# Column-group matmuls recorded as one scheduled piece, and a new list of steps, in a two-layer flow block

## The chip, the cores and the metric

The kernel runs on one core of one Trainium2 chip. The metric is the device time of one execution in microseconds (us), as the median of several runs; a profile of one execution, with every instruction's start and end, stands beside it.

## What is computed

Two layers of a block that works on 512 latent tokens and 256 context tokens of width 1024. Each layer modulates its input with rows that it makes from a condition vector (adaln), projects it to 2464 columns, sends these through four mixers (a gated convolution, latent attention, grouped attention, retention), projects back, and runs an MLP with squared ReLU. Only the latent tokens come out.

```python
def adaln(cond, w, b):
    m = (jax.nn.silu(cond) @ w + b).reshape(cond.shape[0], N_MOD, D_MODEL)
    return tuple(m[:, i, None, :] for i in range(N_MOD))

def grouped_attention(q, k, v):          # per block of 128 queries
    ...
        s = jnp.einsum('bkgqd,bksd->bkgqs', qblk, k, preferred_element_type=jnp.float32) * scale
        p = jax.nn.softmax(s, axis=-1)
        return jnp.einsum('bkgqs,bksd->bkgqd', p.astype(v.dtype), v)

def reference(...):
    for layer in range(DEPTH):           # DEPTH = 2
        last = layer == DEPTH - 1
        sh1, sc1, g1, sh2, sc2, g2 = adaln(c, w_mod[layer], b_mod[layer])
        csh1, csc1, cg1, csh2, csc2, cg2 = adaln(c_ctx[None, :], w_mod[layer], b_mod[layer])
        y_ctx, y_lat = mixing_sublayer(modulate(cx, csh1, csc1), modulate(x, sh1, sc1), ...)
        x = x + g1 * y_lat
        x = x + g2 * sq_relu_mlp(modulate(x, sh2, sc2), mlp_w1[layer], mlp_w2[layer])
        if not last:
            cx = cx + cg1 * y_ctx
            cx = cx + cg2 * sq_relu_mlp(modulate(cx, csh2, csc2), mlp_w1[layer], mlp_w2[layer])
    return rms_norm(x, final_g)
```

In the second layer no context output is needed. Everything is fp32 on the outside.

## The kernel before

Most products are made of three fp32r matmuls: an operand is split into a high and a low part (`split`), and `mm3` adds high x low, high x high and low x high in PSUM. A few products stay plain fp32. These are the ones that the change touches:

- **Modulation rows** (`mod_rows`, called for the first rows of layer 0 by `mods` and, inside layer 0's mixing, through the list `todo` by `later`). The stationary operand is `sf`, 128x32: the two condition vectors for one block of 128 inputs, padded. The contraction over 1024 inputs is 8 such blocks; they go in two sets of four, and the four of a set write to four different groups of 32 output partitions (32 array columns each) of one PSUM tile. The moving operand is a slice of `w_mod`, 256 or 512 columns wide. For 512 columns a set's weights come as two loads of 0.5 MB, two blocks each, into a class of buffers of which there are three (`raw`, `nraw = 3`).
- **Joins of attention** (`Duo.finish`). A `Duo` is a pair of heads for a pair of token tiles. `scores(k)` makes the scores of head k and their softmax, `turn(k)` transposes the probabilities on TensorE and copies them to `pts`, `finish` multiplies them with the values: for each of 6 key tiles (2 for context queries) one matmul for each head, head 0 to output partitions 0 to 63 and head 1 to 64 to 127. The units (`s_units`, `u` in the list) run a Duo's scores while the Duo before is joined.
- **Retention** (`s_ret`). In each of two pairs of heads, for each direction and segment, four fp32 matmuls with the states (128 columns) and then 8 matmuls of 64 columns, two heads by turns, in one PSUM tile.

What sets the order: no engine instruction is issued where it is written. `Plan.record` notes each as an operation with its engine (or several possible engines), a cost and its dependencies, and `Plan.schedule` then runs a list scheduling on these costs: each engine takes the ready operation that was recorded earliest, as long as buffers are free. `Plan.issue` writes the engines' programs in that order. The order of recording inside the mixing of a layer comes from the list `ORDER`: words such as `u:2` (two steps of the generator of units), `taps:4` (four taps of the convolution), `ln`, `read` (norm and readout of convolution and retention), `todo:1` (one modulation row). On a chip each engine works through its own program in order, and waits where an operand is not there.

Since every operation of `Plan` is issued on one line, nearly all instructions of the profile carry the line L646. In names, `b` is one of four PSUM tiles of 512 columns, `pp` one of two pairs of them, `m` a page of SBUF.

Of the kernel before, what the change touches and what calls it, by code (L numbers as in the profile page):

```python
# [66 lines left out]
class _Engine:  # L67
# [5 lines left out]
    def __getattr__(self, fn):  # L73
        return lambda *a, **k: self._p.record(self._n, self._r, fn, a, k)

# [35 lines left out]
class Plan:  # L111
# [7 lines left out]
    def __init__(self, tc, caps, arenas, names):  # L119
        nc = tc.nc  # L120
        self.tc, self.caps, self.arenas, self.names = tc, caps, arenas, names
        self.ahead, self.patience, self.lag = ahead, patience, 0
        self.hurry, self.bias = hurry, {"V": bV, "S": bS, "G": bG}
        self.V, self.S, self.G, self.T, self.D = [_Engine(self, n, e) for n, e in (
            ("V", nc.vector), ("S", nc.scalar), ("G", nc.gpsimd), ("T", nc.tensor), ("D", nc.sync))]
        self.ops, self.tiles = [], {}
        self.masks, self.open = {}, {}
# [66 lines left out]
    def record(self, eng, real, fn, args, kw):  # L194
        alt_kw = kw.pop("alt_kw", None) or {}
        op = _Op()
# [8 lines left out]
        for k, a in kw.items():  # L205
            if hasattr(a, "tensor"):
                (outs if k in ("out", "accum_out") else ins).append(a)
        op.alts = {}
        for e in eng:
            f = fn[e] if isinstance(fn, dict) else fn  # L210
            k = alt_kw.get(e, kw)
            op.alts[e] = (getattr(real[e] if isinstance(real, dict) else real, f), self._cost(e, f, outs, ins, k), k)
# [55 lines left out]
    def _cost_(self, eng, fn, outs, ins, kw):  # L268
# [6 lines left out]
        if eng == "D":  # L275
            big = max(n(a) * a.ap[0][1] for a in outs + ins)
            return max(big * 4 / 290.0, 60.0)
        size = n(outs[0])
        psum = any(self.tiles[a.tensor.name]["psum"] for a in outs[:1] + ins if a.tensor.name in self.tiles)
        if eng == "T":  # L280
            if fn == "transpose":
                return 109.0 if ins[0].ap[0][1] > 16 else 27.0
            if ins[0].dtype == F32:
                if ins[0].ap[-1][1] <= 64:
                    return 4 * size / 2.4 * ins[0].ap[-1][1] / 128
# [395 lines left out]
def block_kernel(ctx: ExitStack, tc: tile.TileContext, x, c, cx, c_ctx, w_mod, b_mod, w_in, w_out,  # L681
# [3 lines left out]
    nc = tc.nc  # L685
# [106 lines left out]
    def mod_rows(l, i, c0, w):  # L792
# [8 lines left out]
        for k0 in range(0, KT, 4):  # L801
# [5 lines left out]
            for k in range(4):  # L807
                T.matmul(o[32 * k:32 * k + 32], lhsT=sf[:, k0 + k], rhs=rs[k // nk][:, k % nk], start=k0 == 0, stop=k0 > 0)
# [152 lines left out]
    def mixing(l, ht, yt, todo, late=None):  # L961
# [64 lines left out]
        class Duo:  # L1026
# [43 lines left out]
            def finish(self):  # L1070
# [3 lines left out]
                for j in range(n):  # L1074
                    for k in range(2):
                        T.matmul(o[64 * k:64 * k + 64], lhsT=self.vst[k](self.kts[j]), rhs=self.pts[k][j // 2][:, j % 2],
                                 start=j == 0, stop=j == n - 1)
# [356 lines left out]
        def s_ret():  # L1434
# [4 lines left out]
            for e in range(2):  # L1439
# [41 lines left out]
                for seg in segs:  # L1481
                    for d in range(2):
                        o = psG(nm="oret")
                        if seg == 0:
                            for c in range(4):
                                cs = slice(c * 128, (c + 1) * 128)
                                T.matmul(o[:, cs], lhsT=states[d][c][:, 2 * e:2 * e + 2].rearrange("p h e -> p (h e)"),
                                         rhs=qdec[d][:, cs], start=c == 0, stop=False)
                        mine = [[x for x in dts if x[0:3] == (d, seg, 2 * e + k)] for k in range(2)]
                        for i, both in enumerate(zip(*mine)):  # L1490
                            for k, (_, _, h, t, a, b, m) in enumerate(both):
                                T.matmul(o[64 * k:64 * k + 64, a:b], lhsT=tile_of(ur, t)[:, 256 + h * 64:320 + h * 64], rhs=m,
                                         start=seg == 1 and i == 0, stop=i == len(mine[0]) - 1)
# [311 lines left out]
```

## Time and profile before

| what | us |
|---|---|
| median of 3 runs | 1684.92 |
| lowest, highest | 1681.69, 1686.33 |
| the profiled execution | 1679.99 |
| its span, first to last instruction | 1678.3 |
| TensorE busy in the span | 1630.6 |
| VectorE busy | 1234.1 |
| ScalarE busy | 569.9 |
| GpSimd busy | 256.0 |

The stages, as TensorE goes through them: start and projections up to 225 us, layer 0's attention and retention with the `todo` rows from about 185 to 410 us, output projection and MLP to about 1100, layer 1's attention in 1167:1264, and the rest. A row of the table of stages has the stretch, its length, and for each engine the busy time in it. A row of the timeline has the start, the time for which the merged instructions were busy, and what they are; the start of the next row tells when TensorE could go on, since matmuls overlap at their ends.

### The profile page before, as it was taken

What the parts mean: (1) busy time and instruction counts of PE and PEld (TensorE: products, weight loads), DVE (VectorE), ACT (ScalarE), POOL (GpSimd) and SP (SyncE); (2) the same over time, 40 slices, a digit from 0 to 9 for tenths busy, and PEclk for the clock granted to TensorE, in tenths of its full rate; (3) what the DMA queues carried; (4) which work ended last, traced back from release to release, by engine and by line L of the source; (5) the groups of instructions that cost most, each with busy time, mean ns of one, the idle gap of its engine ahead of it and who ended that gap; (6) DMA issues with size and microseconds to landing.
All of it is one profiled execution on the core that took longest, in us unless ns stands there. A gap on an engine that the chain in (4) does not pass through costs nothing. (4 is left out here: it accounts for less than half of the span.)

```text
span 1678.3 us, 22457 instructions
## 1 busy us (share of the span) xinstructions
PE 1630.6 (97%) x8603; PEld 1337.5 (80%) x8603; DVE 1234.1 (74%) x2093; ACT 569.9 (34%) x1008; POOL 256.0 (15%) x274
## 2 busy tenths in 40 slices
PE   6999999979999999999999999999989999999997
PEld 4888875657888888888888889788768888888886
DVE  5669956686876978767765667698888766666665
ACT  4431555474351111211211126345472512212212
POOL 2121102143010000010000013303032100000001
PEclk9999999999999999999999999999999999999999
DMA  8412126332322443534421212111125232333331
GB/s 298 135 51 58 51 79 181 102 114 88 98 79 88 127 141 96 164 112 126 151 63 51 74 51 86 46 53 33 53 76 169 83 101 91 98 100 94 95 100 51
DMA packets 138906, 164.03 MB, mean 98 GB/s; under 512 B 7466, under 2 KB 94106, under 8 KB 138800
## 3 DMA queue, kind: packets, MB, share of 16 engines
q1 hardware_dynamic: 138800, 162.61, 31.7%
q8 instruction: 67, 1.10, 0.3%
q14 instruction: 39, 0.32, 0.1%
HBM read 156.56 MB, written 2.10 MB: 95 GB/s over the span
## 5 line engine op out<-in xcount | busy, mean ns | idle before, releaser
L646 PE MATMUL b<-m,m 128*128 128x512 f32 (+5 forms) x6468 | 1316.5, 368 | 8.5 <-DVE m L646 5.8
L646 PEld LDWEIGHTS b<-m,m 128*128 128x128 f32 (+1 forms) x6468 | 1083.1, 185 | 221.8 <-DVE m L646 10.9
L646 DVE TENSOR_TENSOR m<-m,m 128x512 f32<-128x512 f32 (+5 forms) x510 | 457.8, 913 | 69.9 <-PE b L646 56.2
L646 ACT CAST m<-m 128x1024 fp32r<-128x1024 f32 (+3 forms) x219 | 197.4, 916 | 616.7 <-PE b L646 443.7
L646 DVE TENSOR_TENSOR m<-b,m 128x512 f32<-128x512 f32 (+9 forms) x309 | 183.1, 606 | 134.9 <-PE b L646 115.6
L646 POOL TENSOR_TENSOR m<-m,m 128x1024 fp32r<-128x1024 f32 (+5 forms) x67 | 130.3, 1949 | 821.0 <-ACT m L646 449.9
L646 PE MATMUL pp<-m,m 128*128 128x512 f32 (+8 forms) x876 | 180.7, 350 | 3.6 <-ACT m L646 1.9
L646 PEld LDWEIGHTS pp<-m,m 128*128 128x128 f32 (+2 forms) x876 | 134.1, 182 | 37.5 <-issue 11.4
L646 DVE TENSOR_TENSOR m<-m 128x512 f32<-128x512 f32 (+1 forms) x100 | 59.2, 592 | 95.1 <-ACT m L646 94.8
L646 PE MATMUL b<-ident,m 128*128 128x128 f32 (+3 forms) x740 | 109.1, 283 | 12.6 <-DVE m L646 9.1
L646 PEld LDWEIGHTS b<-ident,m 128*128 128x128 f32 (+3 forms) x740 | 86.5, 143 | 35.5 <-DVE m L646 12.1
L646 ACT ACTIVATE m<-b 128x512 f32<-128x512 f32 (+1 forms) x115 | 60.9, 532 | 140.6 <-PE b L646 136.3
L646 DVE SCALAR_TENSOR_TENSOR m<-m,sf,m 128x1024 f32<-128x1024 f32 x80 | 101.8, 1284 | 7.5 <-DMA m<-in_w_mod_dram 7.4
L646 DVE SCALAR_TENSOR_TENSOR m<-m,cvw,m 128x783 f32<-128x783 f32 (+1 forms) x120 | 102.0, 896 | 0.4
L646 ACT COPY m<-b 128x512 f32<-128x512 f32 (+4 forms) x109 | 57.2, 542 | 112.3 <-PE b L646 110.3
L646 DVE TENSOR_REDUCE ty<-pp 128x1 f32<-128x768 f32 (+1 forms) x70 | 62.9, 906 | 12.1 <-PE pp L646 10.8
L646 ACT ACTIVATE m<-pp,ty 128x768 f32<-128x768 f32 (+1 forms) x70 | 60.4, 865 | 31.4 <-DVE ty L646 22.1
L646 DVE CAST m<-m 128x512 fp32r<-128x512 f32 (+4 forms) x126 | 58.9, 471 | 7.5 <-PE b L646 2.6
L646 POOL TENSOR_TENSOR ty<-ty,mhalf 128x1 f32<-128x1 f32 (+4 forms) x47 | 56.3, 1202 | 3.1
L646 ACT ACTIVATE m<-m 128x1024 f32<-128x1024 f32 (+4 forms) x65 | 42.3, 654 | 38.0 <-DVE m L646 37.5
L646 DVE TENSOR_SCALAR m<-m,ty 128x512 f32<-128x512 f32 (+3 forms) x94 | 45.0, 512 | 11.6 <-POOL ty L646 10.9
L646 POOL TENSOR_SCALAR ty<-ty 128x2 f32<-128x2 f32 (+4 forms) x43 | 12.6, 292 | 229.4 <-ACT m L646 163.6
(109 smaller groups left out, 620.8 us busy)
## 6 DMA issues: line engine op xcount, KB each, us to landing
m<-in_mlp_w_dram SPq DMA_DIRECT2D x128, 512.0 KB
m<-in_w_mod_dram SPq DMA_DIRECT2D x96, 512.0 KB
m<-in_w_in_dram SPq DMA_DIRECT2D x32, 512.0 KB
m<-in_w_out_dram SPq DMA_DIRECT2D x16, 512.0 KB
m<-in_x_dram SPq DMA_DIRECT2D x8, 512.0 KB
m<-in_w_in_dram SPq DMA_DIRECT2D x8, 416.0 KB
m<-m SPq DMA_DIRECT2D x24, 96.0 KB
m<-in_ctx_dram SPq DMA_DIRECT2D x4, 512.0 KB
```

Source lines behind the costliest of these rows:

```text
L646: op.fn(*[f(a) for a in op.args], **{k: f(a) for k, a in op.kw.items()})
```

## The change

Three calls now hand a whole group of matmuls to one new operation, `burst`: a set of four in `mod_rows`, a whole join in `finish`, and the twelve (or four) matmuls of one direction and segment in `s_ret`. `Plan.record` takes the operands of all of them as the dependencies of one operation, `Plan` costs it as 94 ns and the sum of its parts, and nothing else can be scheduled between its matmuls. The work itself, 8147 matmuls, is the same. The list `ORDER` is new for both layers; of it one line stands here.

```diff
 ORDER = (
-    "um:2 ug:2 um mla:2 ug gqa:2 a:6 gqa mla a ur:4 taps:2 u:1 ur u:1 gates:2 u:1 gates:2 taps:2 gates "
+    "um:4 ug:2 um ug:2 mla:2 ug gqa:1 a:2 gqa:1 a:4 gqa mla a ur:2 u:1 ur taps:2 u:1 gates:2 taps:4 u:1 "
...
+class _Tensor(_Engine):
+    def burst(self, mms):
+
+        def go(mms):
+            for o, l, r, start, stop in mms:
+                self._r.matmul(self._p.bind(o), lhsT=self._p.bind(l), rhs=self._p.bind(r), start=start, stop=stop)
+
+        return self._p.record(self._n, self._r, go, (), {"mms": mms})
...
+        for o, l, r, _, _ in kw.get("mms", ()):
+            outs.append(o)
+            ins += [l, r]
...
+            call = f if callable(f) else getattr(real[e] if isinstance(real, dict) else real, f)
+            op.alts[e] = (call, self._cost(e, f, outs, ins, k), k)
...
+        if "mms" in kw:
+            return 94 + sum(4 * n(o) / 2.4 * l.ap[-1][1] / 128 for o, l, _, _, _ in kw["mms"])
...
-                if ins[0].ap[-1][1] <= 64:
-                    return 4 * size / 2.4 * ins[0].ap[-1][1] / 128
...
-            for k in range(4):
-                T.matmul(o[32 * k:32 * k + 32], lhsT=sf[:, k0 + k], rhs=rs[k // nk][:, k % nk], start=k0 == 0, stop=k0 > 0)
+            T.burst([(o[32 * k:32 * k + 32], sf[:, k0 + k], rs[k // nk][:, k % nk], k0 == 0, k0 > 0) for k in range(4)])
...
-                for j in range(n):
-                    for k in range(2):
-                        T.matmul(o[64 * k:64 * k + 64], lhsT=self.vst[k](self.kts[j]), rhs=self.pts[k][j // 2][:, j % 2],
-                                 start=j == 0, stop=j == n - 1)
+                T.burst([(o[64 * k:64 * k + 64], self.vst[k](self.kts[j]), self.pts[k][j // 2][:, j % 2], j == 0, j == n - 1)
+                         for j in range(n) for k in range(2)])
...
+                        T.burst(mms)
                         VS.copy(out=oT[d][e][seg], in_=o[:, 0:(512, 256)[seg]])
```

**A set of four in layer 0's mixing.** TensorE's program, the eighth of the twelve sets of 32x512 of `mod_rows`; `sf` is the stationary operand, `m_5602` and `m_5654` are the two loaded halves, the `pp` rows are scores of a unit. Before:

```order
L646 MATMUL b_3212<-m_5602,sf 32x512
L646 MATMUL pp_5687<-m_5242,m_5512 128x512
L646 MATMUL pp_5687<-m_5218,m_5512 128x512 x2
L646 MATMUL pp_5687<-m_5218,m_5512 128x256 x3
L646 MATMUL b_3212<-m_5602,sf 32x512
L646 MATMUL b_3214<-ident,m_4637 128x128 x2
L646 MATMUL pp_5391<-m_4637,m_5398 128x256
L646 MATMUL b_3212<-m_5654,sf 32x512
```

Its fourth matmul follows thirteen instructions later. The same set in the changed program, behind the last matmul of a join and ahead of scores:

```order
L82 MATMUL b_3215<-m_5669,m_4078 64x256
L82 MATMUL b_3212<-m_5593,sf 32x512 x2
L82 MATMUL b_3212<-m_5655,sf 32x512 x2
L661 MATMUL pp_5689<-m_5367,m_5553 128x512 x2
L661 MATMUL pp_5689<-m_5367,m_5553 128x256 x3
```

The four matmuls stand together now, with both halves.

**A join.** TensorE's program, the first join of layer 0 (context queries, so 4 matmuls); the rows between are the gates' projection and scores, both into `pp` tiles. Before:

```order
L646 MATMUL b_3213<-ident,m_4902 128x128
L646 MATMUL b_3212<-m_4867,m_3996 64x256
L646 MATMUL pp_4974<-m_4822,m_3490 128x512
L646 MATMUL pp_4974<-m_4580,m_3490 128x512
L646 MATMUL pp_4974<-m_4580,m_3512 128x512
L646 MATMUL pp_4985<-m_4752,m_4872 128x512
L646 MATMUL pp_4985<-m_4739,m_4872 128x512
L646 MATMUL b_3212<-m_4867,m_3996 64x256 x3
L646 MATMUL pp_4974<-m_4822,m_3490 128x512
```

In the changed program:

```order
L661 MATMUL pp_4993<-m_4697,m_4884 128x512
L661 MATMUL pp_4993<-m_4684,m_4884 128x512 x2
L661 MATMUL pp_4993<-m_4684,m_4884 128x256 x3
L82 MATMUL b_3215<-m_4877,m_4078 64x256 x4
L661 MATMUL b_3212<-m_4824,m_3492 128x512
```

The first matmul of the join no longer stands ahead of the other three.

**The loads of the sets.** SyncE's queue in layer 0's mixing, where loads of `w_mod` meet the copies of retention's operands (`32x768`, from page to page of SBUF). Before:

```order
L646 DMA m_5602<-in_w_mod_dram 128x2x512
L646 DMA m_5654<-in_w_mod_dram 128x2x512
L646 DMA m_5667<-in_w_mod_dram 128x2x512
L646 DMA m_5702<-m_5623 32x768
L646 DMA m_5710<-in_w_mod_dram 128x2x512
L646 DMA m_5702<-m_5623 32x768
```

In the changed program:

```order
L661 DMA m_5714<-in_w_mod_dram 128x2x512
L661 DMA m_5720<-in_w_mod_dram 128x2x512
L661 DMA m_5793<-in_w_mod_dram 128x2x512
L661 DMA m_5804<-in_w_mod_dram 128x2x512
L661 DMA m_5850<-m_5799 32x768 x2
L661 DMA m_5861<-m_5799 32x768
```

The copies come four loads later than they did.

## Rows read from the trace of the kernel before

**Rows 1.** The page: engine's busy time, share of the span, instructions.

```profile
span 1678.3 us, 22457 instructions
PE 1630.6 (97%) x8603; PEld 1337.5 (80%) x8603; DVE 1234.1 (74%) x2093; ACT 569.9 (34%) x1008; POOL 256.0 (15%) x274
```

**Rows 2.** Stages: length, busy PE, PEld, DVE, ACT, POOL, then clock, DMA share, GB/s.

```profile
225.00:330.00 105.00, 104.44 (x672) 64.76 (x672) 68.61 (x165) 54.48 (x122) 15.20 (x22) 1.00 0.49 145
330.00:393.00 63.00, 52.93 (x337) 38.78 (x337) 54.53 (x112) 49.48 (x88) 35.26 (x38) 0.97 0.25 85
1167.00:1264.00 97.00, 91.40 (x654) 70.17 (x652) 83.59 (x172) 64.77 (x123) 23.93 (x28) 1.00 0.22 69
```

**Rows 3.** TensorE's waits over the span: total us, times, longest.

```profile
PE b L646 <- DVE m L646: 14.9, 15, 2.9
...
PE b L646 <- DVE cvw L646: 0.2, 1, 0.2
```

**Rows 4.** Groups of TensorE by form: count, busy us, mean ns, idle before.

```profile
L646 PE MATMUL b<-m,m 128*64 128x256 f32 x372 | 58.5, 391 | 0.3 <-DVE m L646 0.3
...
L646 PE MATMUL b<-m,m 128*64 128x128 f32 x76 | 7.4, 280 | 0.0
...
L646 PE MATMUL pp<-m,m 128*64 128x128 f32 x68 | 6.3, 281 | 0.0
```

**Rows 5.** Timeline of TensorE, slots of 32x512: start, busy us, what.

```profile
275.69 1.04 PE L646 MATMUL b<-m,sf 128*32 128x512 f32 x2
276.67 0.44 PE L646 MATMUL b<-ident,m 128*128 128x128 f32 x2
...
290.49 1.06 PE L646 MATMUL b<-m,sf 128*32 128x512 f32 x6
```

**Rows 6.** Timeline of TensorE, slots of 32x256 near the start.

```profile
41.60 1.07 PE L646 MATMUL b<-m,sf 128*32 128x256 f32 x16
...
44.12 0.63 PE L646 MATMUL b<-m,sf 128*32 128x256 f32 x4
```

**Rows 7.** Timeline of TensorE, joins (128*64) and transposes beside them.

```profile
266.44 0.88 PE L646 MATMUL pp<-ident,m 128*128 128x128 f32 x6
267.25 0.65 PE L646 MATMUL b<-m,m 128*64 128x256 f32 x2
267.82 0.33 PE L646 MATMUL b<-ident,m 128*128 128x128 f32 x1
...
268.31 0.60 PE L646 MATMUL b<-ident,m 128*128 128x128 f32 x4
268.75 0.38 PE L646 MATMUL pp<-ident,m 128*128 128x128 f32 x2
...
282.12 2.80 PE L646 MATMUL b<-m,m 128*64 128x256 f32 x22
...
342.02 2.81 PE L646 MATMUL b<-m,m 128*64 128x256 f32 x24
344.76 0.50 PE L646 MATMUL pp<-m,m 128*128 128x512 f32 x1
```

**Rows 8.** Timeline of TensorE, a stretch of retention in layer 1.

```profile
1186.57 1.96 PE L646 MATMUL pp<-m,m 128*64 128x128 f32 x28
```

**Rows 9.** Timeline of TensorE in layer 1's attention, with waits in brackets.

```profile
1224.56 0.63 PE L646 MATMUL b<-ident,m 128*128 128x128 f32 x4 [0.77 <-DVE m L646]
1225.86 0.66 PE L646 MATMUL b<-ident,m 128*128 128x128 f32 x4 [0.68 <-ACT m L646]
...
1226.88 0.65 PE L646 MATMUL b<-m,m 128*64 128x256 f32 x2
```

**Rows 10.** Timeline of SyncE's queue: the issue of a load of a half.

```profile
232.27 0.37 SPq L646 DMA_DIRECT2D m<-in_w_mod_dram  x1
```

**Rows 11.** Stage view just behind it; last columns: DMA share, GB/s.

```profile
234.00:235.60 1.60, 1.52 (x10) 1.40 (x11) 1.19 (x6) 1.44 (x4) 0.00 (x0) 1.00 0.71 255
235.60:240.00 4.40, 4.40 (x35) 2.99 (x33) 2.07 (x5) 2.34 (x5) 0.00 (x0) 1.00 0.00 1
```

More of the change, by code (lines that the diff above doesn't have):

```diff
@@ L123, in __init__ @@
         self.hurry, self.bias = hurry, {"V": bV, "S": bS, "G": bG}
-        self.V, self.S, self.G, self.T, self.D = [_Engine(self, n, e) for n, e in (
-            ("V", nc.vector), ("S", nc.scalar), ("G", nc.gpsimd), ("T", nc.tensor), ("D", nc.sync))]
+        self.V, self.S, self.G, self.D = [_Engine(self, n, e) for n, e in (
+            ("V", nc.vector), ("S", nc.scalar), ("G", nc.gpsimd), ("D", nc.sync))]
+        self.T = _Tensor(self, "T", nc.tensor)
         self.ops, self.tiles = [], {}
@@ L211, in record @@
             k = alt_kw.get(e, kw)
-            op.alts[e] = (getattr(real[e] if isinstance(real, dict) else real, f), self._cost(e, f, outs, ins, k), k)
+            call = f if callable(f) else getattr(real[e] if isinstance(real, dict) else real, f)
+            op.alts[e] = (call, self._cost(e, f, outs, ins, k), k)
         op.port = {e: self._port(e, fn[e] if isinstance(fn, dict) else fn, outs, alt_kw.get(e, kw)) for e in eng}
@@ L1483, in s_ret @@
                         o = psG(nm="oret")
+                        mms = []
                         if seg == 0:
@@ L1486, in s_ret @@
                                 cs = slice(c * 128, (c + 1) * 128)
-                                T.matmul(o[:, cs], lhsT=states[d][c][:, 2 * e:2 * e + 2].rearrange("p h e -> p (h e)"),
-                                         rhs=qdec[d][:, cs], start=c == 0, stop=False)
+                                mms.append((o[:, cs], states[d][c][:, 2 * e:2 * e + 2].rearrange("p h e -> p (h e)"),
+                                            qdec[d][:, cs], c == 0, False))
                         mine = [[x for x in dts if x[0:3] == (d, seg, 2 * e + k)] for k in range(2)]
@@ L1491, in s_ret @@
                             for k, (_, _, h, t, a, b, m) in enumerate(both):
-                                T.matmul(o[64 * k:64 * k + 64, a:b], lhsT=tile_of(ur, t)[:, 256 + h * 64:320 + h * 64], rhs=m,
-                                         start=seg == 1 and i == 0, stop=i == len(mine[0]) - 1)
+                                mms.append((o[64 * k:64 * k + 64, a:b], tile_of(ur, t)[:, 256 + h * 64:320 + h * 64], m,
+                                            seg == 1 and i == 0, i == len(mine[0]) - 1))
+                        T.burst(mms)
                         VS.copy(out=oT[d][e][seg], in_=o[:, 0:(512, 256)[seg]])
```

10 rows, old and new, of the table ORDER are left out of this document.

## Prediction

> **What bounds the kernel now.** I read the page's busy shares first, then the stage table, then the waits. TensorE is busy for 1630.6 us of a span of 1678.3 [rows 1]; VectorE follows with 74%. By stage [rows 2], at a granted clock of 0.97 to 1.00 of full speed, TensorE is busy nearly all the time in 225:330 (104.4 of 105), and it waits in two places: the end of layer 0's attention (52.9 of 63) and layer 1's attention (91.4 of 97). Its waits are 38.2 us in all, in eight kinds of which [rows 3] show the largest and the smallest; 10.0 and 5.6 of them lie in these two tails. So a microsecond of TensorE work taken out of a full stage is a microsecond of the span; one taken out beside a wait may only lengthen the wait.
>
> The change is about fp32 matmuls that fill only 32 or 64 columns of the array. The trace holds two records for each fp32 matmul (a join of 12 matmuls is x24 in [rows 7]), and I halve counts accordingly. The largest group of them is busy for 58.5 us [rows 4]; the question is how much of this is cut-up work.
>
> **The change part by part.**
>
> *Sets of four, 32x512.* Layer 0's mixing makes six modulation rows from 12 sets of four matmuls. A slot with one such matmul (x2) runs from 275.69 to 276.67, 0.98 us; a slot with three of them (x6) is busy for 1.06, where one is busy for 1.04 [rows 5]. So one and three cost the same, and a fourth lies beside them: with 256 columns a slot of two matmuls (x4) is busy for 0.63 and two whole sets (x16) for 1.07 [rows 6], so a whole set adds 0.5 where a half alone costs 0.55 (a slot's busy time ends 0.07 after the next start). The order of before cuts the 12 sets into 24 slots: each half has a load of its own and starts with it, and some halves are cut again by a join or by scores. The changed order has 12 slots. Saved: 12 x 0.98 = 11.8 us. All of them stand between 225 and 310 us, where TensorE has next to no idle time [rows 2], so this lies on the path.
>
> *Joins of a pair of heads, 64x256.* There are 20, sixteen of 12 matmuls and four of 4. A whole one of 12 takes 2.74 us (342.02 to 344.76); eleven (x22) are busy as long as twelve, 2.80 and 2.81; one alone takes 0.57 (267.25 to 267.82) [rows 7]. All of this is about 0.15 us for a piece and 0.43 for each pair begun. By the order of before 17 of the 20 have their first matmul standing alone, 13 of them with the rest in one piece: 13 x 0.58 = 7.5 us. The four others stand in pieces of 1,1,2,5,3, of 1,1,10 (two) and of 1,3,5,3: by the same rule 1.46 + 2 x 0.73 + 1.31 = 4.2 us over a whole one. Saved: 11.7 us.
>
> *The ends of a stretch.* Six transposes between two column-group stretches take 0.81 us (266.44 to 267.25), four undisturbed ones 0.44 (268.31 to 268.75), 0.11 each [rows 7]: the two ends cost 0.81 - 0.66 = 0.15. The order has 83 stretches of fp32 matmuls before and 45 after (13, 43 and 27 at the start, in layer 0, in layer 1; then 11, 23 and 11). 38 x 0.15 = 5.7 us.
>
> *Sets of 32x256 at the start.* Four halves stand alone where two whole sets would do: 2 x 0.55 = 1.1 us [rows 6].
>
> *Retention.* A stretch of 14 matmuls of 64x128 is busy for 1.96 us, 0.27 a pair [rows 8]. The 36 pairs would be 9.7 us, against 13.7 for which their two groups are busy [rows 4]; single matmuls and the overlap of the groups make up the difference. I take 3, between 1 and 4.
>
> Gross: 11.8 + 11.7 + 5.7 + 1.1 + 3 = 33 us, between 31 and 36 (the bounds of retention, and the ends at up to 0.2 beside other neighbours than transposes).
>
> *The list of steps.* From TensorE's instruction 1919 (410 us) to 5449 (1101 us) and over the last 1561 (from 1324 us) the two orders have the same instructions one by one, so nothing is to be won or lost there. The new list acts inside 159:410 and 1101:1279, with small shifts at 34:122. In layer 0 the norm of the convolution and the first output projections come earlier among the units; in layer 1 eleven instructions leave VectorE. I cost the list at nothing, with the bounds +10 (the waits of layer 0's tail come a second time) and -6 (four tenths of both tails' waits go): the chain scores, softmax, transposes, join stays as long as it is, and only the work between its links is dealt anew.
>
> *A new wait.* A piece begins when its last operand is there: a join's twelve now wait for the last of the transposed probabilities, and behind them TensorE's whole queue. Before, the first matmul of a join ran early, and in the tails it did so beside waits: one stands at 1226.88, 1 us behind waits of 0.77 and 0.68 [rows 9]. What is saved there need not be won. In 1167:1264 the sum above takes away some 8.5 us (4.9 joins, 2.4 ends, 1.2 retention): TensorE's work falls from 91.4 to 83, and VectorE's is 83.6 in 97 [rows 2]. Two engines of equal load that hand work to each other do not both run full; at 90%, between the 94% that TensorE reaches there and the 87% of layer 0's tail's VectorE, the stage takes 92. So of 8.5 I count 5 and lose 3.5; 0.5 goes to loads (below). In layer 0's tail about 4 us are saved, and I let the earlier norms pay for what VectorE (54.5 of 63) can't follow.
>
> Net: 33 - 4 = 29 us. The profiled execution took 1679.99 us (span 1678.3 and 1.7 around it); the median of the runs is 1684.92, 4.9 more. An execution like the profiled one comes to 1651; the median would be 1656 and, with the ends at 0.2 (2 us) and a little of the list's upside, which I think likelier than its downside since it fills the tail with ready projections, 1653.
>
> **The rivals.**
>
> *VectorE takes over.* In 225:330 VectorE is at 68.6 and ScalarE at 54.5 of 105 [rows 2], so there is room even at 85 us; in both tails VectorE is at 86%. Then the tails give nothing back (8.5 + 4 of the 33) and the list costs up to 6: 15 to 20 us saved, 1665 to 1670. Against it: all the sets and the larger part of the stretches lie in the roomy stage. The Trainium skill, "TensorEngine Tiling (Array Packing)", section "Performance Considerations", has this as a rule: tiling speeds up TensorE but not the emptying of PSUM, which may then become the bottleneck.
>
> *The list gains as well.* The tails' 15.6 us of waits shrink by 6 or more and the gross sum is at 36: 1640 to 1645. For it: projections that are ready earlier fill the tails. Against it: the links of the attention chain.
>
> *Nothing is won.* This holds if the early pieces only filled time that must be waited out anyway. The rows speak against it: in 225:330 TensorE is idle for 0.6 us in all [rows 2].
>
> *Slower: sets wait for loads.* A set now needs both halves, and there are three buffers for halves: the second half of a set is fetched only when the set before has run. A load of 0.5 MB issued at 232.27 [rows 10] has stopped moving bytes at 235.6 [rows 11], 3.3 us later. The changed order has 3 to 8 us of TensorE work between one set and the next, so that two or three sets may wait half a microsecond: the 0.5 above. If loads took 9 us, because retention's 24 small copies share the queues (the DMA share of 225:330 is 0.49 already), each of ten sets would wait 4 us, 40 in all, and the kernel would end at 1690 to 1695. It decides from about 8 us a load, where it eats the 33. Against it: 21 of the 24 loads now stand ahead of the first copy in SyncE's queue, 17 before.
>
> **How the numbers follow.** A measurement of this kernel can tell 0.3%, 5 us. Forecast (1646 to 1661) 0.60; VectorE takes over (1661 to 1676) 0.17; the list gains too (1638 to 1646) 0.16; nothing won (within 5 us of 1685) 0.04; loads (slower) 0.03. The range 1642 to 1668 takes in the bounds of the sum (31 to 36 gross, most of +10 to -6 for the list) and leaves out the far ends of the second and third case and the last two. Faster 0.93, same 0.04, slower 0.03.
>
> **What would show it.** TensorE busy for about 1597 us; the groups of 32x512 near 12 us and those of 64x256 near 51; no join piece of 0.57 left. No wait for w_mod of over 1 us in layer 0. Waits of TensorE between 28 and 45 us in all; at 50 or more, with VectorE as releaser, it took over; with a w_mod load as releaser, the last rival holds. I am wrong at the root if a whole set of four 32x512 takes more than 1.1 us.

## The result, and the profile after

The changed kernel takes 1642.28 us (median of 4 runs, 1641.05 to 1642.95) where the kernel before takes 1683.87 in the same comparison: a ratio of 0.975, 95% interval 0.973 to 0.977. The forecast was 1653 (1646 to 1661, within a range of 1642 to 1668). The gain, 42 us, is larger than the 32 forecast: the time lies at the very edge of the range, in the band of the rival that the list gains as well, to which 0.16 was given. The profiled execution took 1641.05 us.

The page of the changed kernel, first lines (span; busy time, share and instructions of each engine), answers [rows 1]:

```profile
span 1639.2 us, 22449 instructions
PE 1597.8 (97%) x8603; PEld 1328.3 (81%) x8603; DVE 1227.0 (75%) x2091; ACT 571.6 (35%) x1015; POOL 232.5 (14%) x269
```

TensorE has 32.8 us less to do than before (1630.6); 1597 was expected. The rest of the 39 us by which the span became shorter is nearly all waiting time, and this is what the forecast had with the wrong sign. TensorE's waits after (total us, times, longest) answer [rows 3], where they were 38.2 in all:

```profile
PE b L661 <- DVE m L661: 13.0, 19, 2.9
PE b L82 <- DMA m<-in_w_mod_dram: 4.8, 3, 4.2
PE b L661 <- ACT srow L661: 4.4, 1, 4.4
PE pp L661 <- DVE m L661: 3.5, 6, 0.9
PE pp L661 <- ACT m L661: 3.3, 8, 0.7
PE b L661 <- ACT m L661: 2.0, 4, 0.7
PE b L82 <- DVE m L661: 1.0, 3, 0.4
```

That is 32.0 us, 6.2 less than before: 3.3 of it in layer 0's attention stage, 1.1 in layer 1's and 1.5 in the MLP between them. The new operation has the line L82; only its waits are the new wait of the prediction, and but for the load at the start (4.2 at once) they come to 1.6 us.

The groups of narrow fp32 matmuls (count of records, two for each matmul; busy us, mean ns; idle before) answer [rows 4]:

```profile
L82 PE MATMUL b<-m,m 128*64 128x256 f32 x408 | 48.9, 384 | 0.7 <-DVE m L661 0.7
L82 PE MATMUL b<-m,sf 128*32 128x512 f32 x96 | 13.8, 605 | 0.5 <-DVE m L661 0.3 <-DMA m<-in_w_mod_dram 0.2
L82 PE MATMUL b<-m,m 128*64 128x128 f32 x112 | 8.1, 278 | 0.0
L82 PE MATMUL pp<-m,m 128*64 128x256 f32 x24 | 2.8, 384 | 0.0
L82 PE MATMUL pp<-m,m 128*64 128x128 f32 x32 | 2.2, 279 | 0.0
```

The groups of 64x256, nearly all of them joins, are busy for 51.7 us (near 51 expected), retention's pairs for 10.3 (13.7 before, so 3.4 saved where 3 were taken), the sets of 32x512 for 13.8 (near 12 expected). The timeline of TensorE shows a whole join and a whole set back to back, and the one set that fell in two (start, busy us, what; answers [rows 5, 7]):

```profile
275.47 2.81 PE L82 MATMUL b<-m,m 128*64 128x256 f32 x24
278.21 1.06 PE L82 MATMUL b<-m,sf 128*32 128x512 f32 x8
279.21 0.70 PE L661 MATMUL pp<-m,m 128*128 128x256 f32 x2
...
289.87 1.05 PE L82 MATMUL b<-m,sf 128*32 128x512 f32 x4
291.11 1.05 PE L82 MATMUL b<-m,sf 128*32 128x512 f32 x4 [0.20 <-DMA m<-in_w_mod_dram]
```

A set of four takes 1.00 us (278.21 to 279.21), as one matmul of it did alone. In the last set the second half's load was late by 0.20; its first two matmuls ran alone and took a slot of their own. So there are 13 slots of 1.06, hence 13.8.

Now the two attention stages, between the starts of the same matmuls of TensorE's program (columns as in [rows 2]). Layer 0's from its first matmul to the 1919th, and layer 1's from the 5449th to the 6588th; before:

```profile
159.20:410.60 251.40, 240.77 (x1425) 171.45 (x1425) 187.33 (x360) 141.16 (x273) 58.20 (x63) 0.99 0.32 99
...
1100.60:1323.60 223.00, 215.05 (x1294) 173.41 (x1294) 190.89 (x334) 113.17 (x204) 54.75 (x51) 1.00 0.23 71
```

and after:

```profile
155.90:381.50 225.60, 218.32 (x1427) 166.04 (x1425) 190.98 (x365) 131.19 (x264) 49.02 (x62) 1.00 0.35 112
...
1069.90:1284.00 214.10, 207.33 (x1295) 171.18 (x1294) 183.87 (x327) 124.29 (x218) 43.58 (x47) 1.00 0.24 71
```

Layer 0's stage became 25.8 us shorter, of which TensorE's work is 22.5; layer 1's became 8.9 shorter, of which work is 7.7. In neither did VectorE become the bound: it is busy for 85% and 86% of the two stages after (75% and 86% before). On balance nothing that was saved went into new waits.

### The profile page after: what moved, and what is told of

Its sections match the earlier page's. It is cut to its first block, busy times and chain, and to the rows that moved or that the text cites. A ratio compares the mean times of both kernels' runs of the same rounds, so it can differ in the third digit from the quotient of the medians.

```text
span 1639.2 us, 22449 instructions
## 1 busy us (share of the span) xinstructions
PE 1597.8 (97%) x8603; PEld 1328.3 (81%) x8603; DVE 1227.0 (75%) x2091; ACT 571.6 (35%) x1015; POOL 232.5 (14%) x269
## 5 line engine op out<-in xcount | busy, mean ns | idle before, releaser
L661 PE MATMUL b<-m,m 128*128 128x512 f32 (+3 forms) x6013 | 1253.2, 369 | 4.2 <-DVE m L661 2.7
L661 PEld LDWEIGHTS b<-m,m 128*128 128x128 f32 (+1 forms) x6013 | 1047.3, 189 | 195.5 <-DVE m L661 9.6
L661 DVE TENSOR_TENSOR m<-m,m 128x512 f32<-128x512 f32 (+7 forms) x516 | 458.7, 904 | 68.5 <-PE b L661 54.3
L661 DVE TENSOR_TENSOR m<-b,m 128x512 f32<-128x512 f32 (+8 forms) x320 | 187.6, 600 | 121.8 <-PE b L661 99.2
L661 PE MATMUL pp<-m,m 128*128 128x512 f32 (+6 forms) x697 | 157.6, 362 | 4.0 <-DVE m L661 2.0
L661 PEld LDWEIGHTS pp<-m,m 128*128 128x128 f32 (+1 forms) x697 | 118.4, 189 | 30.6 <-ACT m L661 6.4
L661 DVE TENSOR_TENSOR m<-m 128x256 f32<-128x256 f32 (+2 forms) x105 | 63.4, 604 | 100.3 <-ACT m L661 100.1
L661 PE MATMUL b<-ident,m 128*128 128x128 f32 (+3 forms) x762 | 108.1, 278 | 11.4 <-DVE m L661 10.3
L82 PE MATMUL b<-m,m 128*64 128x256 f32 (+2 forms) x568 | 61.6, 354 | 0.7 <-DVE m L661 0.7
L661 DVE CAST m<-m 128x512 fp32r<-128x512 f32 (+3 forms) x119 | 55.2, 467 | 7.9 <-PE b L661 2.1
L82 PEld LDWEIGHTS b<-m,m 128*64 128x64 f32 (+1 forms) x568 | 39.5, 141 | 18.5 <-issue 2.4
```

Source lines behind the costliest of these rows:

```text
L82: self._r.matmul(self._p.bind(o), lhsT=self._p.bind(l), rhs=self._p.bind(r), start=start, stop=stop)
L661: op.fn(*[f(a) for a in op.args], **{k: f(a) for k, a in op.kw.items()})
```

## The experiments

All the times stand in one table. The stages, waits and spells of a kernel are those of its one profiled execution. The stages are cut at the starts of the same four places of TensorE's program (its matmuls 733, 1919, 5449 and 6588; at the first a few instructions may stand on the other side); "rest" goes from the last of them to the start of TensorE's last matmul, some 9 us before the end of the span. "Waits" are TensorE's in the two attention stages; "half clock" is the number and total length of the spells (stretches of time), before the last 10 us, in which the granted clock of TensorE was 0.50 or 0.51, so at 1.2 instead of 2.4 GHz. The ratio is to the kernel before in the same comparison. In the MLP's stage before, after, l0new, tail0new and head0new have the same sequence of matmul shapes on TensorE, and it took 687.2 to 690.5 us: some 3 us in one stage need not come from the change.

| kernel | median us | ratio [95%] | start | layer 0 | MLP | layer 1 | rest | waits L0, L1 | half clock |
|---|---|---|---|---|---|---|---|---|---|
| before | 1683.87 | 1 | 159.2 | 251.4 | 690.0 | 223.0 | 345.5 | 10.6, 7.9 | 1: 3.4 |
| after | 1642.28 | 0.975 [0.973, 0.977] | 155.9 | 225.6 | 688.4 | 214.1 | 346.2 | 7.3, 6.8 | none |
| burst_oldlist | 1656.68 | 0.985 [0.981, 0.989] | 156.6 | 234.5 | 689.0 | 218.0 | 345.8 | 11.9, 9.3 | 2: 10.2 |
| newlist_noburst | 1683.91 | 1.000 [0.998, 1.002] | 160.0 | 247.0 | 692.8 | 229.6 | 346.0 | 8.1, 11.1 | 5: 17.1 |
| sets_oldlist | 1666.26 | 0.990 [0.987, 0.993] | 156.4 | 240.7 | 689.6 | 222.4 | 345.8 | 11.2, 8.0 | 2: 6.8 |
| joins_oldlist | 1666.32 | 0.990 [0.987, 0.993] | 157.5 | 240.3 | 691.9 | 218.7 | 346.0 | 12.8, 8.8 | 3: 13.7 |
| l0new | 1648.88 | 0.978 [0.976, 0.981] | 157.3 | 225.3 | 690.5 | 220.0 | 346.3 | 7.4, 9.8 | 1: 3.4 |
| l1new | 1652.34 | 0.980 [0.978, 0.983] | 157.5 | 234.2 | 688.8 | 214.1 | 346.1 | 12.1, 6.7 | 2: 6.8 |
| tail0new | 1646.48 | 0.976 [0.974, 0.978] | 158.2 | 227.5 | 687.2 | 214.9 | 346.1 | 10.1, 7.7 | none |
| head0new | 1644.43 | 0.975 [0.973, 0.977] | 155.9 | 226.8 | 687.4 | 214.8 | 346.2 | 9.5, 7.5 | none |
| nosets_newlist | 1649.87 | 0.979 [0.976, 0.981] | 159.7 | 232.7 | 685.8 | 214.5 | 346.0 | 8.1, 7.1 | none |
| nojoins_newlist | 1664.32 | 0.988 [0.985, 0.991] | 156.8 | 242.7 | 687.3 | 221.0 | 345.8 | 13.6, 7.0 | 2: 6.8 |
| relist | 1644.12 | 0.974 [0.972, 0.976] | 159.5 | 229.1 | 686.9 | 213.2 | 345.9 | 8.4, 6.1 | 2: 6.8 |
| honest_before | 1725.73 | 1.024 [1.021, 1.026] | 165.4 | 281.2 | 691.2 | 230.2 | 345.8 | 28.4, 14.3 | 8: 34.1 |

**Pieces without the list, and the list without pieces.** The change has two parts, so each was run alone. burst_oldlist is the changed kernel with the list of before:

```diff
 ORDER = (
-    "um:4 ug:2 um ug:2 mla:2 ug gqa:1 a:2 gqa:1 a:4 gqa mla a ur:2 u:1 ur taps:2 u:1 gates:2 taps:4 u:1 "
+    "um:2 ug:2 um mla:2 ug gqa:2 a:6 gqa mla a ur:4 taps:2 u:1 ur u:1 gates:2 u:1 gates:2 taps:2 gates "
...
```

> The three groups as one piece each, with the list of steps of before. By the durations of before's rows its 45 stretches take 107 us where before's 83 take 143 (35.6 less). Theory A (the pieces win TensorE's work, the new list wins the waits): TensorE busy 1597 to 1598, waits of TensorE 38 or more, as before; time 33 to 36 us under before. Theory B (the pieces themselves take the waits away, since the planner now costs what it really issues): waits 33 or less, time 39 to 42 under before, as the changed kernel. Theory C (the old list does not suit the pieces, joins wait for their last operand): waits over 45, time 20 to 28 under before.

newlist_noburst is the kernel before with the new list, the same lines the other way round.

> The new list of steps with the matmuls recorded one by one as before. Its stretches are 80 and take 138 us by before's rows, 4 less than before. Theory A: the list takes waits away by itself: waits 30 to 33 of TensorE's, time 8 to 11 us under before. Theory B: the list alone is worth the 4 us of fewer cuts and nothing in waits: 2 to 5 us under before. Theory C: a list made for other costs is worse: waits over 42, time equal to before or above.

Measured: the pieces alone gain 28 us, the list alone gains nothing (interval 0.998 to 1.002), both together 42. So the two are not a sum: the list is worth 14 us with the pieces and none without. None of the expectations fits whole. burst_oldlist has the time of its theory C (20 to 28 us gained) without the waits of over 45 us; newlist_noburst gains less than B (0.6 us, not 2 to 5) without the waits of over 42 us that C asked for. The nothing of the list alone is itself a sum: between the two profiles layer 0's stage is 4.4 us shorter, layer 1's 6.6 longer with three of the five spells. As the profiled execution of newlist_noburst was the longest of its ten (1686.87), the loss is put too high by that. The page of burst_oldlist and that of newlist_noburst, TensorE's line:

```profile
PE 1603.4 (97%) x8603; PEld 1330.9 (81%) x8603; DVE 1225.2 (74%) x2080; ACT 577.4 (35%) x1017; POOL 254.6 (15%) x280
```

```profile
PE 1636.2 (97%) x8603; PEld 1342.8 (80%) x8603; DVE 1237.0 (73%) x2097; ACT 573.6 (34%) x1008; POOL 235.2 (14%) x273
```

Beside the changed kernel (1597.8 busy, 32.0 waited), burst_oldlist is busy 5.6 us longer and waits 8 longer. Its first wait rows are

```profile
PE b L661 <- DVE m L661: 15.4, 20, 2.9
PE b L661 <- POOL m L661: 6.9, 2, 4.5
PE pp L661 <- DVE m L661: 5.0, 7, 1.5
```

and all eight kinds come to 40.1. (4.5 of the 6.9 us for GpSimd are one wait at the start, where the changed kernel waits 4.4 for ScalarE; the other is the 2.41 below.) The larger busy time is for the most part not more work, since the same pieces run, but the half clock. In its timeline, the same form of 12 matmul records once behind the wait for GpSimd and once later:

```profile
321.39 2.93 PE L661 MATMUL b<-m,m 128*128 128x256 f32 x12 [2.41 <-POOL m L661]
...
359.52 1.67 PE L661 MATMUL b<-m,m 128*128 128x256 f32 x12 [0.65 <-DVE m L661]
```

and the stretches around the two spells (columns as above; the clock is the third number from the end):

```profile
314.30:320.00 5.70, 3.99 (x30) 3.07 (x30) 5.61 (x14) 5.55 (x11) 0.93 (x3) 0.99 0.00 0
320.00:326.80 6.80, 5.41 (x21) 5.02 (x22) 5.48 (x12) 3.45 (x6) 3.62 (x4) 0.51 0.00 0
346.50:350.70 4.20, 1.25 (x10) 0.78 (x8) 4.20 (x5) 1.88 (x5) 3.50 (x3) 0.99 0.36 110
350.70:354.00 3.30, 3.25 (x15) 2.12 (x16) 2.64 (x8) 2.49 (x5) 1.06 (x2) 0.50 0.05 19
```

The 8.7 us of work in the two spells (5.41 + 3.25) would take half at 2.4 GHz, so about 4 of the 5.6 us are the clock's. Ahead of each spell TensorE stood idle for a good part of the stretch. The spells are not one execution's: the mean granted clock was 0.995 in all four runs of burst_oldlist and 0.998 or 0.999 in those of the changed kernel.

**One kind of piece alone, with the old list.** In sets_oldlist only `mod_rows` uses a piece, in joins_oldlist only `finish`; the other two calls are as before, and the cost line of narrow matmuls is back for them:

```diff
             if ins[0].dtype == F32:
+                if ins[0].ap[-1][1] <= 64:
+                    return 4 * size / 2.4 * ins[0].ap[-1][1] / 128
                 return max(4 * size, 256) / 2.4 + 7
```

> Only the sets of four of the modulation rows as one piece, old list. Its 71 stretches take 127 us, 16 less than before (11.8 for slots, the rest for ends and halves at the start). Theory A: 14 to 17 us under before, waits as before, no wait of over 1 us for a w_mod load in layer 0. If sets wait for their second half (the slower rival), waits for w_mod of 0.5 us or more at several of the twelve sets, and less than 12 us gained.

> Only the joins of attention as one piece, old list. Its 54 stretches take 119 us, 23.5 less than before by the rows (joins 12, ends, and sets that are cut less as nothing of a join stands between). Theory A: 20 to 24 us under before. If a join's early single matmul only filled waits in the tails, 12 to 17, with waits of TensorE 43 or more.

Measured: 1666.3 both, 18 us each; a little above the 14 to 17 expected of the sets, and between the two cases for the joins (20 to 24, or 12 to 17 with waits of 43 us or more; the waits were 42.8). The sets gain in layer 0 (10.7 us of its stage) and at the start (2.8), and nothing that matters in layer 1 (0.6), where there are none. The joins gain in both stages, 11.1 and 4.3. The two gains, 36 us, are more than the 28 of all the pieces with this list; both alone and together they leave the waits of layer 0's stage at 11 to 13 us, above the 10.6 of before. So with the old list the pieces save work as forecast, and some of it returns as waits and half clock (with all the pieces and this list busy time fell by 27.2 us, not by 33).

**The new list in one layer.** l0new and l1new have all the pieces, and the new list for one layer:

> All three kinds of pieces; the new list for layer 0 alone, the old one for layer 1. Two runs bound it: pieces with the old list came to 1656.7 us, with the new one to 1642.3. Theory D (the list's 14 us are made of local gains, each in its layer): by the stages of these two profiles 8.9 us of them lie in layer 0's attention (234.5 to 225.6 us), 0.7 at the start and 3.9 in layer 1's attention, so 1656.7 - 9.6 = 1647 us, between 1645 and 1649, and the stage of layer 0's attention near 225.6 us. Theory E (chance: any other order of the same instructions falls otherwise among waits and spells of the half clock, so a mixed list may land anywhere): outside 1645 to 1649, and layer 0's stage 3 us or more away from 225.6.

> All three kinds of pieces; the new list for layer 1 alone, the old one for layer 0. Theory D (local gains): 1656.7 - 3.9 - 0.2 = 1652.5 us, between 1650 and 1655, with layer 0's attention at 234.5 us as with the old list in both layers, its waits (11.9 us) and its spells of the half clock (some 3 us of TensorE time) again, and layer 1's attention near 214. Theory E (chance): outside that; if layer 0's stage alone differs from 234.5 by over 3 us although its list is the same, then the stage isn't set by its list.

Measured: 1648.88 and 1652.34, and the stages answer more sharply than the times: layer 0's is 225.3 us with the new list and 234.2 with the old one, whatever layer 1 has (225.6 and 234.5 in the two kernels above); layer 1's is 214.1 and 220.0 (214.1 and 218.0 above). The gain is local and repeats, as theory D had it; the times fall into its ranges too. Layer 0's part is about 9 us, layer 1's 4 to 6; the 2 us between the two values of the old list in layer 1 are nearly all one spell of the half clock, which l0new has there and burst_oldlist has not (shown in the last section). In l1new the wait of 2.41 us for GpSimd stands again, at the same place of the old list:

```profile
323.02 1.79 PE L661 MATMUL b<-m,m 128*128 128x256 f32 x12 [2.41 <-POOL m L661]
```

**Which half of layer 0's list.** The prediction had seen a possible gain in the tail (earlier norm and readout). tail0new takes the old words up to `rin` and the new ones behind it; head0new the other way round; layer 1 has the new list.

```diff
-    ... todo:4 todo:5 u:1 taps:7 rin u:1 ret u:2 taps u:2 ln u:3 read:1 u:2 read:1 u:1 read u "
+    ... todo:4 taps:6 todo:5 taps:4 rin u:1 ret u:2 taps u:2 ln u:3 read:1 u:2 read:1 u:1 read u "
```

> All pieces, the new list in layer 1; in layer 0 the old words up to and with rin, the new ones behind it (ret, the last taps, ln, read and the last units). With the old words for all of layer 0 the time was 1652.3 us and its attention stage 234.2 us; with the new ones 1642.3 and 225.6. Theory T (the earlier norm of the convolution, readout and output projections among the last units fill the tail, as the prediction supposed): nearly the whole 10 us, 1643 to 1646, stage 225 to 228. Theory H (the gain comes from the words ahead: in which order units, modulation rows, gates and taps stand up to 310 us): little, 1650 to 1653, stage 232 or more.

> All pieces, the new list in layer 1; in layer 0 the new words up to and with rin, the old ones behind it. Theory T (the tail's words make the gain): 1650 to 1653, layer 0's attention stage 232 us or more, waits of TensorE in it near 12 us. Theory H (the words ahead make it): 1643 to 1646, stage 225 to 228, waits near 7. If both parts give half, about 1647 here and in the other half, or neither gives anything alone (both near 1652), since the head decides which unit meets which word of the tail.

Measured: 1646.48 and 1644.43, ratios 0.976 and 0.975, which can't be told from the whole new list's 0.975; the stages are 227.5 and 226.8. Neither of the two theories holds: either half gives nearly all of it. Both halves were expected to give half each, or neither anything alone, as a third outcome; that they overlap was not foreseen. So it is not the new list that has something special: the old head followed by the old tail is the odd pair, the only one of four that leaves layer 0 at 234 us. Neither half-new kernel has a wait for GpSimd of over 1.05 us in the tail or a spell of the half clock, though both wait longer than the changed kernel (10.1 and 9.5 us in the stage). head0new even has the longest single wait of all of them there, with no spell behind it (the second row is the stretch 310 to 385 us, with a granted clock of 1.00):

```profile
332.65 1.66 PE L657 MATMUL b<-m,m 128*128 128x256 f32 x12 [3.34 <-DVE m L657]
...
310.00:385.00 75.00, 67.39 (x456) 53.26 (x451) 60.35 (x122) 53.68 (x101) 36.74 (x38) 1.00 0.20 64
```

**The new list with one kind of piece missing.** In nosets_newlist the sets are recorded matmul by matmul again, in nojoins_newlist the joins; the cost line of narrow matmuls, shown above, is back for them in both. The edit of the first:

```diff
-            T.burst([(o[32 * k:32 * k + 32], sf[:, k0 + k], rs[k // nk][:, k % nk], k0 == 0, k0 > 0) for k in range(4)])
+            for k in range(4):
+                T.matmul(o[32 * k:32 * k + 32], lhsT=sf[:, k0 + k], rhs=rs[k // nk][:, k % nk], start=k0 == 0, stop=k0 > 0)
```

> The changed kernel with the sets of four recorded matmul by matmul again; joins and retention stay pieces, the new list stays. By the stretches of fp32 matmuls in its order, priced by the rows of before, TensorE has 8.7 us more work than in the changed kernel. If the list keeps its 14 us of gain beside two kinds of pieces: 1642.3 + 8.7 = 1651. If the gain needs all three (the planner's picture is wrong as soon as one kind of narrow matmul is costed below what the chip takes): 1651 + 14 = 1665. In between: the gain depends on where the wrongly costed matmuls stand; the sets are all ahead of layer 0's tail, so I expect more than half of it gone, 1658 to 1663.

> The changed kernel with the joins of attention recorded matmul by matmul again; sets and retention stay pieces, the new list stays. By the stretches in its order, priced by the rows of before, TensorE has 15.8 us more work than in the changed kernel. If the list keeps its gain: 1642.3 + 15.8 = 1658. If the gain needs all three kinds: 1658 + 14 = 1672. The joins stand in both tails, where the waits are, so I expect most of the gain gone, about 1670, with waits of 38 us or more and spells of the half clock again.

Measured: without sets 1649.87, as if the list kept its whole gain (1651), against my leaning (1658 to 1663); without joins 1664.32, between keeping (1658) and losing it (1672). The rows of waits tell the same: 15.2 us in the two stages without the sets (14.1 in the changed kernel), 20.6 without the joins. By these sums, which rest on 8.7 and 15.8 us of estimated work, the list keeps its gain without whole sets and about half of it without whole joins. That fits where they stand: the sets run where TensorE is full anyway, the joins are links of the chain in the tails.

**A third list.** relist has all pieces and other lists for both layers (gates and a modulation row earlier, the last units in longer runs).

> The changed kernel with a third list for both layers: gates and a modulation row earlier among the units of layer 0, the last units in runs of five in layer 0 and three to five in layer 1 ahead of the last readout. The pieces are the same, so TensorE's work is 1597 to 1600 us. If a list made for the pieces is worth what the new one is (its gains lie in waits of the tails and spells of the half clock), and this one shortens the tails' waits a little further: 1638 to 1642. If the tails' waits are at the floor that the chain scores, softmax, transposes, join sets (14 us in both attention stages together in the changed kernel): 1642 to 1645. If lists scatter by chance on the chip: 1645 to 1655.

Measured: 1644.12, a ratio of 0.974 [0.972, 0.976], the same as the changed kernel's. Layer 1's stage is 213.2 us, layer 0's 229.1 with two spells. That is the expectation of a floor (1642 to 1645) and not the hoped-for 1638 to 1642. It doesn't beat the changed kernel; for five lists of layer 0 with the pieces the stage is 234.2 to 234.5 (old), and 225.3 to 229.1 (four others).

**The price instead of the piece.** honest_before is the kernel before with one line of the planner changed, so that a lone narrow matmul costs what it takes alone:

```diff
                 if ins[0].ap[-1][1] <= 64:
-                    return 4 * size / 2.4 * ins[0].ap[-1][1] / 128
+                    return 4 * size / 2.4 + 150
```

> The kernel before, no pieces and its old list; only the planner's cost of a matmul of 32 or 64 columns is raised from 213 ns to the slot that it takes on the chip when it stands alone (0.57 us for 64x256, about 1 us for 32x512). It tells whether the pieces gain because the planner then sees their true price, or because nothing comes between their matmuls. Theory P (price): the waits of layer 0's tail shrink and TensorE loses little to cut-up work, 1670 to 1675. Theory Q (what counts is that nothing comes between): the order still has 77 stretches of fp32 matmuls where the kernel before has 83 and the pieces have 45, worth 2.5 us by the rows of before, so 1680 to 1686, no difference that can be told.

Measured: 1725.73, slower by 2.4% (interval 2.1 to 2.6%). Neither theory's time came. TensorE's waits rise from 38.2 to 66.9 us, with loads of `w_mod` among them (in the two attention stages they more than double), and most of layer 0's stage (the last row) runs at a mean clock of 0.94:

```profile
PE b L646 <- DVE m L646: 23.8, 24, 3.5
PE b L646 <- DMA m<-in_w_mod_dram: 14.6, 11, 4.6
...
225.00:410.00 185.00, 161.05 (x964) 106.72 (x963) 120.36 (x268) 94.60 (x197) 23.50 (x41) 0.94 0.35 111
```

The line prices each matmul of a set at a slot of its own, about 1 us, so a set of four is planned at 4 us, and takes 1.0 where its four do stand together; a matmul costed singly can't be priced right in both cases. A join of twelve is planned at 6.9 us (12 x 577 ns) in the same way, where a whole one takes 2.74. So this run tries a price that is too high, and not a fair one; no run has the pieces without their price or a better price without the pieces. That the plan's error is what makes the waits here is my reading; the run shows only that the price of these few matmuls alone moves the kernel by 39 us (against 1687.08 in its comparison), through waits (28.7 us more) and clock (31 us more of spells) and hardly through work.

## Why the prediction was right and where it was wrong

**The work: right.** Gross 33 us were forecast, TensorE's busy time fell by 32.8. Some 1.7 of these are the one spell of the half clock in the profile of before (half of its 3.4 us, below), so the work itself fell by about 31. By terms, in busy time of the groups: the sets of 32x512 25.9 (two groups of before, 18.7 and 7.2) to 13.8, so 12.1 for 11.8; retention 3.4 for 3. The joins' groups fell by 18.1 (69.8 to 51.7), which holds the joins' 11.7 and most of the ends' 5.7, as records overlap their neighbours there; the runs don't separate the two. The halves of 32x256 fell by 1.3 (12.4 to 11.1) for 1.1. The premise that a set of four costs what one matmul costs holds: 1.00 us.

**The loads: right in kind.** One set waited 0.20 us for its second half, and being cut by it cost a slot more, so 1.2 us where 0.5 was charged. It also shows that a piece does not begin only when its last operand is there, as I had put it: the planner counts so, but on the chip two matmuls of this set ran ahead of the second half's load. The rival with loads of 9 us did not come.

**The new wait: a size too large, and in the wrong place.** I charged 3.5 us in layer 1's tail, from two engines of nearly equal load that can't both run full. TensorE kept its share of the time there (207.33 of 214.10 us, 97%; 96% before), so the stage gave back 7.7 us of work and 1.2 of waits. What I had wrong here is the 90% that I let TensorE reach beside VectorE's 83.6 us in 97 [rows 2]; VectorE stood at 86% of the whole stage both before and after, and TensorE reached 97% beside it. With the old list the charge was about right: layer 1's stage fell by 5.0 us there (223.0 to 218.0), near the "5 of 8.5", and its waits rose from 7.9 to 9.3 (in l0new, with a spell there, it fell by 3.0). The Trainium skill, "TensorEngine Tiling (Array Packing)", section "Performance Considerations", warns that the emptying of PSUM may become the bottleneck once tiling has made TensorE faster. In this kernel it did not: TensorE's waits for VectorE fell from 20.5 us over the span (14.9 + 5.4 + 0.2 in three kinds) to 17.5 (13.0 + 3.5 + 1.0), although VectorE's share of layer 0's stage rose from 75% to 85%.

**The list at nothing: the step that failed.** Its bounds were +10 and -6, and it was worth -14 beside the pieces (1656.68 to 1642.28). As TensorE's orders were the same outside the two attention stages, but for small shifts at the start, I was right to look for it only there, and the l0new and l1new runs confirm it. The mistake was to judge the list as a thing by itself, a deal of the work between the links of a chain that stays as long as it is. By itself it is worth nothing indeed (ratio 1.000), though as a gain in layer 0 and a loss in layer 1. With the pieces, the old list leaves layer 0's tail with the 2.41 us wait for GpSimd and several around 1 to 1.7, and the half clock comes on top: over the whole span about 8 us of waits and 4 of clock more than the new list. Of the four other lists of layer 0, all wait less in its stage (7.3 to 10.1 against 12) and three have no spell in it. For the pieces alone the sum was near: 1656 before the 3 us taken off for the upsides, 1656.68 measured. That is partly luck: the profiled execution took 1654.5 where the sum had 1651, since busy time fell by 27.2 and not by 33 (part of the difference is the half clock), and waits rose by 1.9 where 4 was charged; and the median stood 2.2 above it, not 4.9.

**The clock: not in the sum.** The prediction named clocks of 0.97 to 1.00 and gave them no term. One spell of the kernel before, 3.4 us at 369 us, is gone in the changed one, and the old list with pieces had three times that. The stretch of the spell of before, with TensorE busy all through and a granted clock of 0.51:

```profile
369.40:372.80 3.40, 3.40 (x14) 1.94 (x13) 2.51 (x4) 1.20 (x3) 1.69 (x4) 0.51 0.02 5
```

In the medians the clock weighs more than these profiles tell. The profiled execution of before had a mean granted clock of 0.998; 13 other runs of it had 0.993 to 0.998, with 0.995 in the middle, and the longest and the shortest of them lie at the ends (1689.87 us at 0.993, 1677.78 at 0.998). The four of the changed kernel had 0.998 or 0.999. By these figures I estimate that some 5 us of the 42 are the clock's (0.003 of 1680).

**The rivals.** *VectorE takes over* did not happen. *The list gains as well* gave 1640 to 1645, and the time is in it; but its reason, projections that are ready earlier fill the tail, is only half of it: with the new words ahead of `rin` alone and the old tail, the time is the same. *Nothing won* is refuted by burst_oldlist.

**The arithmetic of the miss.** The profiled execution was put at 1651 and took 1641.05: 10 us, nearly all of it waits and half clock (-6.2 where +4 stood in the sum). The median was put 4.9 above the profiled execution and stood 1.2 above it, which fits the clocks just told, and 3 us had been taken off for the upsides; so 10 + 3.7 - 3 = 10.7 us between 1653 and 1642.3.

**What stays open.** Why the old head and the old tail together are the bad pair: the wait for GpSimd and the spells are there in both kernels that have the pair with all pieces and in neither of the two that have half of it, but no run took that one wait away by itself. Which idle stretches bring a spell of the half clock is open too, and so is what the pieces gain by their price to the planner and what by standing together.

## What to carry to other kernels

Count a column-group matmul by the slot that it takes in the order as issued, not by its own columns: that part of the sum was right to about 2 us of 33. A hand-fitted order and the grain of what it orders belong together: run the new grain with the old order and the new order with the old grain, since here they gave 28 and 0 us and 42 together, and a forecast that costs "the order" at nothing should let its range take in what the new grain does to the waits and the clock. Where a planner costs operations one by one, an operation whose price depends on its neighbours has no single right price; recording it as one piece gained 28 us here, and the one other price that was tried lost 39.

## What the runs showed of the hardware

The granted clock of TensorE fell to half (1.2 GHz) for spells of 3.41 or 6.83 us in the middle of a kernel that is busy for 97%. In newlist_noburst one stands in layer 1's attention, behind waits of which none is over 0.9 us:

```profile
1224.19 0.47 PE L646 MATMUL pp<-m,m 128*128 128x512 f32 x1 [0.90 <-DVE m L646]
...
1225.81 0.63 PE L646 MATMUL b<-ident,m 128*128 128x128 f32 x4 [0.69 <-DVE m L646]
1227.12 1.12 PE L646 MATMUL b<-ident,m 128*128 128x128 f32 x4 [0.68 <-ACT m L646]
1228.03 1.06 PE L646 MATMUL pp<-ident,m 128*128 128x128 f32 x4
```

Four transposes take 0.63 us ahead of the spell and 1.12 within it. The stretches, ahead of it and in it:

```profile
1223.00:1226.90 3.90, 1.84 (x11) 1.13 (x9) 3.73 (x8) 2.07 (x5) 0.00 (x0) 1.00 0.01 2
1226.90:1230.30 3.40, 3.18 (x11) 2.10 (x12) 3.23 (x8) 2.82 (x6) 0.00 (x0) 0.50 0.00 0
```

TensorE was busy for 1.84 of the 3.90 us ahead. But a spell does not follow from such a stretch alone. burst_oldlist and l0new have the same list for layer 1, and the same wait of 1.66 us stands in its tail:

```profile
1212.42 0.44 PE L661 MATMUL b<-ident,m 128*128 128x128 f32 x2 [1.66 <-DVE m L661]
...
1205.98 0.68 PE L661 MATMUL b<-ident,m 128*128 128x128 f32 x2 [1.66 <-DVE m L661]
```

The stretches ahead of its end and behind it, in burst_oldlist and then in l0new:

```profile
1209.00:1212.40 3.40, 1.42 (x9) 0.75 (x7) 3.40 (x11) 3.17 (x5) 2.65 (x6) 1.00 0.01 2
1212.40:1215.80 3.40, 3.18 (x24) 2.75 (x24) 2.72 (x7) 2.95 (x7) 3.16 (x6) 1.00 0.03 5
...
1202.60:1206.00 3.40, 1.39 (x10) 0.73 (x8) 3.40 (x11) 3.21 (x5) 2.65 (x6) 1.00 0.00 0
1206.00:1209.40 3.40, 3.40 (x14) 3.20 (x15) 2.40 (x7) 1.66 (x4) 3.16 (x6) 0.50 0.00 0
```

TensorE was busy for 1.42 and 1.39 of the 3.40 us ahead, and then had the full clock in the one and half of it in the other. The single wait of 3.34 us in head0new brought no spell either. So a wait costs more than its own length where a spell follows it, but neither the length of a wait nor the busy time ahead of it told here whether one would follow.
